# Ten of the MLP's half down projections as Strassen-like block products, and two weight sums made by adding loads

## The chip, the core and the metric

The kernel runs on one core of a Trainium2 chip. The metric is the device time of one execution in microseconds (us). The engines are TensorE (PE, with its weight loads as PEld), VectorE (DVE), ScalarE (ACT), GpSimd (POOL) and SyncE (SP), which starts most loads. All work from queues of their own and wait for each other through semaphores.

## What is computed

The reference is a decoder trunk of two layers on x of 512 positions by 1024 features, in float32:

```
for l in range(2):
    h = rms_norm(x, norm_mix_g[l])
    proj = h @ w_in[l]
    ... differential attention, short convolution, RWKV-7 ...
    x = x + mixed @ w_out[l]
    h = rms_norm(x, norm_mlp_g[l])
    x = x + square(relu(h @ w_mlp_up[l])) @ w_mlp_down[l]
return rms_norm(x, final_norm_g)
```

Only the MLP matters here: 1024 features up to 4096, squared ReLU, and down to 1024.

## The kernel before

Everything is kept transposed: a tile has 128 features on the partitions and the 512 positions along the free dimension. x is eight such tiles that stay in SBUF. To keep float32 precision each product is made of three matmuls: an operand is split into a high part (cast to fp32r) and a low part (the operand less the high part), and high times high, high times low and low times high are summed in PSUM. A weight chunk of 256 KB (four blocks of 128 by 128) is loaded by SP, its high part is cast by ScalarE (L346), its low part subtracted by VectorE (L347).

The MLP of a layer makes 32 "middle" tiles (up projection, ReLU, square) and sums them into x through 64 blocks of the down projection. Four middle tiles are made plainly (`up`), the other 28 in 14 pairs (`two`): a pair takes the tile pair, the two halves of the features and the two halves of the positions as a 2 by 2 block product and makes it from seven products instead of eight, each of 4 blocks by three matmuls of 256 columns, 84 matmuls in all. Products are summed in the PSUM tiles `pa`, `pb`, `pc`. The weight operands of the seven products are w11, w12, w22 and the sums s1 = w21 + w22, s2 = s1 - w11, s3 = w11 - w21, s4 = w12 - s2, made on VectorE (`sum_`, L1484 for the first pair and L1486). Each is split into `shi_p` (ScalarE, L1477) and `slo_p` (VectorE, L1478). The position operands are h's blocks and sums of them, made once a layer (`blocks`).

`square` turns a finished product c into a middle tile: VectorE takes ReLU and the scale of the norm into `r` (L1416), ScalarE squares it into `m` (L1418), ScalarE casts the high part `mh` (L1407), GpSimd subtracts the low part `ml` (L1408; VectorE for the first four).

`down(h, js)` takes the four middle tiles 4h to 4h+3 and four of the eight tiles of x (a half: js is 0 to 3 or 4 to 7): for each of them 4 blocks by three matmuls of 512 columns into a PSUM tile `dn` of two buffers (tag "mm"), and a VectorE add into x (L1554); 48 matmuls a half. After the pairs, one half follows each pair as soon as 4h+6 middle tiles stand, so the program alternates a pair and a half. That alternation is a period. PE's order is the program's; the order of the other engines' instructions is set by a scheduler from what they depend on and when they are due.

The kernel's weights for plain products go through a ring of three buffers (`weights`), and in the MLP every fourth chunk through a spare one.

The MLP starts behind the norm: GpSimd's `rrf` (L371) gives the norm's rates, which PE spreads over the partitions (`prbf`, L285).

Of the kernel before, what the change touches and what calls it, by code (L numbers as in the profile page):

```python
# [10 lines left out]
F32 = mybir.dt.float32  # L11
# [11 lines left out]
S = 512  # L23
P = 128
# [155 lines left out]
NG = NG_IN + NG_OUT + NG_UP + NG_DN  # L180

N_ONE = 4

WHOLE = 5
PT = 1
# [86 lines left out]
def tile_trunk(ctx: ExitStack, tc: tile.TileContext, xT, wts, prm_d, cst_d, lora_d, gup_d, lam_d, fin_d, hd_d, out):  # L272
# [29 lines left out]
    def psum(tag, bufs, name):  # L302
        return ps.tile([P, 512], F32, tag=tag, bufs=bufs, name=name)
# [167 lines left out]
    def last_group(fp, wbase, mids):  # L471
# [24 lines left out]
        def norm(half, sq):  # L496
# [23 lines left out]
            act.copy(rbs, rb[-1][:, :H])  # L520
            os_ = []
            for j in range(NK):
                o = fp.tile([P, H], F32, tag=("p1", "p5", "u2", "c1")[j // 2], bufs=2, name=f"o{half}_{j}")
# [42 lines left out]
    for l in range(L):  # L566
# [825 lines left out]
        acts = [inner[j] for j in range(NK)]  # L1392
        with ExitStack() as mx:
            fp = mx.enter_context(tc.tile_pool(name=f"fp{l}", bufs=1))
            spare[0] = fp
            RING = 10
            H = S // 2
            mids = []
# [3 lines left out]
            def kept(m):  # L1402

                i = len(mids)
                hi = fp.tile([P, S], F32R, tag="mh", bufs=RING, name=f"mh{l}_{i}")
                lo = fp.tile([P, S], F32R, tag="ml", bufs=RING, name=f"ml{l}_{i}")
                act.copy(hi, m)  # L1407
                (dve if i < 4 else pool).tensor_tensor(lo, m, hi.bitcast(F32), ALU.subtract)  # L1408
                mids.append((hi, lo))

            def square(cs, name):

                r = fp.tile([P, S], F32, tag="r", bufs=2, name=f"r{name}")
                for i, c in enumerate(cs):
                    q = slice(i * H, i * H + c.shape[1])
                    dve.scalar_tensor_tensor(r[:, q], c, 0.0, rs[:, q], ALU.max, ALU.mult)  # L1416
                m = fp.tile([P, S], F32, tag="m", bufs=3, name=f"m{name}")
                act.activation(m, r, AF.Square)  # L1418
                kept(m)

            def up(i):

# [23 lines left out]
            def blocks(q):  # L1446
                hi, lo = th[q] = [fp.tile([P, 4, H], F32R, tag=f"t{p}{q}", name=f"t{p}{l}_{q}") for p in ("hi", "lo")]
                for i in range(2):
                    u = slice(2 * i, 2 * i + 2)
                    t = fp.tile([P, 2, H], F32, tag="c0" if q == 1 else ("s3", "s4")[i], bufs=1 + (q == 1), name=f"t{l}_{q}_{i}")  # L1450
                    for k in (2 * i, 2 * i + 1):
                        b1, b2, o = bn[k], bn[k + 4], t[:, k % 2]
                        if q == 0:
                            dve.tensor_tensor(o, b1[:, 1], b1[:, 0], ALU.subtract)
                        elif q == 1:
                            dve.tensor_tensor(o, b2[:, 1], tb[0, i][:, k % 2], ALU.subtract)
                        elif q == 2:
                            dve.tensor_tensor(o, b2[:, 1], b1[:, 1], ALU.subtract)
                        else:
                            dve.tensor_tensor(o, b2[:, 0], tb[1, i][:, k % 2], ALU.subtract)  # L1460
                    tb[q, i] = t
                    act.copy(hi[:, u], t)
                    dve.tensor_tensor(lo[:, u], t, hi[:, u].bitcast(F32), ALU.subtract)

            def two(i0, i1):

# [1 line left out]
                wg = wbase + NG_IN + NG_OUT  # L1468

                def raw(i, a):  # L1470
                    t = fp.tile([P, 4, P], F32, tag="sraw", bufs=6, name=f"raw{n}_{i}_{a}")
# [8 lines left out]

                def sum_(name, a, b, op):
                    t = fp.tile([P, 4, P], F32, tag=name, name=f"{name}{n}")
                    if i0 == N_ONE and name in ("s1", "s3"):
                        dve.scalar_tensor_tensor(t, a, none, b, ALU.add, op)  # L1484
                    else:
                        dve.tensor_tensor(t, a, b, op)  # L1486
                    return t

                def small(name):
                    return fp.tile([P, H], F32, tag=name, bufs=2, name=f"{name}{n}")  # L1490
# [19 lines left out]
                w21 = raw(i1, 0)  # L1510
                w22 = raw(i1, 4)
# [4 lines left out]
                s2 = sum_("s2", s1, w11, ALU.subtract)  # L1516
# [3 lines left out]
                w12 = raw(i0, 4)  # L1520
                product(pc, both(w12, "p2"), blk(1, 0))
                dve.tensor_tensor(c0[:, :H], pc, p1, ALU.add)
                s3 = sum_("s3", w11, w21, ALU.subtract)
                product(pa, both(s3, "p7"), smm(2), False)
# [3 lines left out]
                s4 = sum_("s4", w12, s2, ALU.subtract)  # L1528
                product(pb, both(s4, "p3"), blk(1, 1), False)
                dve.tensor_tensor(c0[:, H:], pb, u2, ALU.add)  # L1530
                square([c0], f"{n}_0")
                product(pa, both(w22, "p4"), smm(3), False)
                square([pa, c1], f"{n}_1")
# [24 lines left out]

            for i in range(N_ONE):
                up(i)  # L1560
            for j in range(NK):
                by_gain(j)
            down(0, range(4))
# [82 lines left out]
```

## Time and profile before

| | |
|---|---|
| median of 3 runs | 1236.34 us (1236.31 to 1236.89) |
| the profiled execution's own time | 1238.42 us |
| its span | 1236.6 us |
| granted TensorE clock, mean | 0.998 |
| busy: PE, VectorE, ScalarE, GpSimd | 1226.2, 934.4, 693.0, 351.7 us |

The profile is one execution. A row of its timeline gives start and duration in us, the engine, the line, the operation, what is written and read by the program's names, the shape, and in brackets how long the engine had been idle and what ended that. The chain of waits follows back from the last instruction what released each step. A window gives the engines' busy time in a stretch. Line 285 is a helper through which all matmuls go, so PE's groups are told by tile.

### The profile page before, as it was taken

The page shows a single profiled execution, that of the slowest core. Times are in us where ns is not written, and L with a number is a line of the kernel's source. Part 1 is how long each engine was busy: PE and PEld are TensorE (multiplying, and loading weights), DVE is VectorE, ACT ScalarE, POOL GpSimd, SP SyncE. Part 2 cuts the span into 40 slices and gives each one's busy share as a digit, 9 for nine tenths or more (in the row PEclk, how much of TensorE's full clock was granted, in tenths as well). Part 3 has the DMA queues.
Part 4 walks back from the last instruction along what each step waited for, and adds up shares of the span by engine and source line. Part 5 has one row for each costly group of instructions (what it writes and reads, how often), then busy time and mean ns, then how long its engine had stood idle before and what let it go on. Part 6 is the DMA issues. An engine that isn't in the chain of part 4 may idle for free.

```text
span 1236.6 us, 25555 instructions
## 1 busy us (share of the span) xinstructions
PE 1226.2 (99%) x9730; PEld 1056.4 (85%) x9730; DVE 934.4 (76%) x1805; ACT 693.0 (56%) x1456; POOL 351.7 (28%) x450
## 2 busy tenths in 40 slices
PE   9999999999999999999999999999999999999997
PEld 7788788888999998989888888888889999998987
DVE  6787888879887676765666777887798867676753
ACT  6785655558455454544465657464775545454542
POOL 2263636341122111120035455464202211111111
PEclk9999999999999999999999999999999999999999
DMA  6523323124433323321235243232433333323121
GB/s 217 165 91 96 111 90 111 54 86 154 143 97 102 103 94 107 99 86 44 69 105 166 77 126 114 88 85 70 152 113 118 106 102 102 104 95 107 55 69 68
DMA packets 84266, 127.94 MB, mean 103 GB/s; under 512 B 21296, under 2 KB 25136, under 8 KB 84144
## 3 DMA queue, kind: packets, MB, share of 16 engines
q1 hardware_dynamic: 83424, 125.57, 32.5%
q8 instruction: 76, 1.25, 0.4%
q10 hardware_dynamic: 720, 0.75, 0.2%
q14 instruction: 46, 0.38, 0.1%
HBM read 117.11 MB, written 9.18 MB: 102 GB/s over the span
## 4 chain that ended last, share of the span: by engine, by line
PE 92%; DVE 2%; ACT 2%; DMA 1%; POOL 1%; issue 1%; SPq 0%; POOLq 0%; ACTq 0%; DVEq 0%
PE dn L285 25%; PE pj L285 21%; PE pa L285 13%; PE po L285 8%; PE pb L285 7%; PE dnF L285 4%; PE pc L285 3%; PE up L285 2%; PE sc L285 1%; PE ptt L290 1%; PE pg L285 1%; PE pyy L285 1%; PE pzw L285 1%; PE pst L285 1%; DMA raw<-wts 0%
## 5 line engine op out<-in xcount | busy, mean ns | idle before, releaser
L1408 POOL TENSOR_TENSOR ml<-m,mh 128x512 fp32r<-128x512 f32 x56 | 90.5, 1634 | 497.5 <-ACT mh L1407 356.5
L285 PE MATMUL dn<-mh,whi 128*128 128x512 f32 x448 | 175.5, 392 | 0.0
L285 PE MATMUL dn<-ml,whi 128*128 128x512 f32 x448 | 175.2, 391 | 0.1
L285 PE MATMUL dn<-mh,wlo 128*128 128x512 f32 x448 | 175.2, 391 | 0.0
L692 POOL TENSOR_TENSOR wlo<-raw,whi 128x512 fp32r<-128x512 f32 x84 | 111.5, 1328 | 210.4 <-ACT whi L680 167.2
L346 ACT CAST whi<-raw 128x512 fp32r<-128x512 f32 x126 | 77.9, 619 | 157.5 <-PE dn L285 147.8
L285 PE MATMUL pj<-ahim,whi 128*128 128x512 f32 x392 | 156.8, 400 | 0.0
L285 PE MATMUL pj<-ahim,wlo 128*128 128x512 f32 x392 | 156.4, 399 | 0.0
L285 PE MATMUL pj<-alom,whi 128*128 128x512 f32 x392 | 155.9, 398 | 0.0
L1554 DVE TENSOR_TENSOR x<-dn,x 128x512 f32<-128x512 f32 x108 | 74.5, 690 | 89.9 <-PE dn L285 89.8
L680 ACT CAST whi<-raw 128x512 fp32r<-128x512 f32 x142 | 87.7, 618 | 71.7 <-PE pj L285 27.5
L1477 ACT CAST shi_p<-s 128x512 fp32r<-128x512 f32 x112 | 69.4, 621 | 78.4 <-PE pa L285 61.9
L347 DVE TENSOR_TENSOR wlo<-raw,whi 128x512 fp32r<-128x512 f32 x126 | 97.3, 774 | 6.1 <-ACT whi L346 6.1
L285 PEld LDWEIGHTS dn<-mh,wlo 128*128 128x128 f32 x448 | 84.2, 188 | 18.5
L285 PEld LDWEIGHTS dn<-ml,whi 128*128 128x128 f32 x448 | 84.2, 188 | 17.7 <-DVE ml L1408 0.5
L285 PEld LDWEIGHTS dn<-mh,whi 128*128 128x128 f32 x448 | 84.1, 188 | 17.4
L285 PE MATMUL pa<-thi,shi_p 128*128 128x256 f32 x336 | 95.1, 283 | 0.0
L285 PE MATMUL pa<-tlo,shi_p 128*128 128x256 f32 x336 | 94.9, 282 | 0.0
L285 PE MATMUL pa<-thi,slo_p 128*128 128x256 f32 x336 | 94.1, 280 | 0.0
L1478 DVE TENSOR_TENSOR slo_p<-s,shi_p 128x512 fp32r<-128x512 f32 x112 | 77.6, 697 | 21.2 <-ACT shi_p L1477 18.4
L285 PEld LDWEIGHTS pj<-alom,whi 128*128 128x128 f32 x392 | 73.9, 188 | 14.0 <-issue 0.5
L285 PEld LDWEIGHTS pj<-ahim,wlo 128*128 128x128 f32 x392 | 73.8, 188 | 13.9 <-issue 0.2
(427 smaller groups left out, 3242.5 us busy)
## 6 DMA issues: line engine op xcount, KB each, us to landing
raw<-wts SPq DMA_DIRECT2D x389, 256.0 KB, 2.6
qs<-dqhi SPq DMA_DIRECT2D x24, 128.0 KB, 3.4
ks<-dkhi SPq DMA_DIRECT2D x24, 128.0 KB, 3.6
x<-xT SPq DMA_DIRECT2D x8, 256.0 KB, 5.0
dqhi<-qhi SPq DMA_DIRECT2D x6, 256.0 KB, 3.4
dqlo<-qlo SPq DMA_DIRECT2D x6, 256.0 KB, 3.4
dkhi<-khi SPq DMA_DIRECT2D x6, 256.0 KB, 3.1
dklo<-klo SPq DMA_DIRECT2D x6, 256.0 KB, 3.5
```

What stands on the lines that cost most here:

```text
L285: ins = nc.tensor.matmul(*a, **k)
L290: ins = nc.tensor.transpose(*a, **k)
L346: act.copy(hi[:, :n], raw[:, :n])
L347: (pool if a and lean[0] else dve).tensor_tensor(lo[:, :n], raw[:, :n], hi[:, :n].bitcast(F32), ALU.subtract)
L680: yield act.copy(hi[:, k0:k1], raw[:, k0:k1])
L692: yield eng.tensor_tensor(lo[:, k0:k1], raw[:, k0:k1], hi[:, k0:k1].bitcast(F32), ALU.subtract)
L1408: (dve if i < 4 else pool).tensor_tensor(lo, m, hi.bitcast(F32), ALU.subtract)
L1477: act.copy(hi, src)
L1478: dve.tensor_tensor(lo, src, hi.bitcast(F32), ALU.subtract)
L1554: dve.tensor_tensor(x[j], pt, x[j], ALU.add)
```

## The change

**The down halves.** In layer 0 the halves of h = 2, 4 and 6, and in layer 1 those of h = 2 and 4, become `quad`s, ten in all. A quad makes two pairs of x tiles; for a pair, the two x tiles, the two pairs of middle tiles (4h, 4h+2 and 4h+1, 4h+3) and the two halves of the positions are the 2 by 2 blocks, and seven products stand for eight, each of 2 blocks by three matmuls of 256 columns: 2 x 7 x 2 x 3 = 84 matmuls a quad. They run into PSUM tiles `qa`, `qb`, `qc`; after each product VectorE adds what stands in the tile into half of an x tile (L1587), and a later product goes on summing in `qa` or `qb`, so x is added to seven times a pair. The weight operands are w0 (a chunk of four blocks), two sums s12 and s34 built on VectorE from two chunks (four rows of 256 columns), and w22 (half a chunk), each split on ScalarE and VectorE (L1574).

**The middle tiles' blocks.** `turn_blocks` makes the sums of middle tiles that a quad needs, after the pair that makes them: four VectorE differences of 256 columns (L1554 to L1557: `ta`, `tb`), a low part of 512 (`dlo`, L1560) and two of 256 (`alof`, L1565), and the casts on ScalarE. It runs after six pairs in layer 0 and four in layer 1.

**The sums s1 and s3** of all 28 pairs are made by loads (`summed`): SP loads one chunk, and GpSimd issues a second load of another chunk into the same tile with an add. They are issued a pair ahead. A pair loads seven chunks then, before it was four. Signs are turned so that s2 and s4 are sums, and the second middle tile of a pair takes min for max.

**Buffers.** `square` writes `m` directly and squares in place, so `r` goes; `m` has four buffers; the spare weight buffers go; `sraw` has five buffers for six, `p5` one for two; the tile `o` of the norm before takes other places for j 2 and 3.

Three places where the order of instructions differs. The first is VectorE, layer 0, around the end of pair 10 and the first tile of the half h = 3. `r0_10` and `m0_10` are pair 10's middle tiles, `slo0_11` and `s30_12` belong to the next pairs, `wlo78_4` is a weight split. Before:

```order
L1416 SCALAR_TENSOR_TENSOR r0_10_0_5867<-c00_10_5743,rsf0_4121 128x512
L1416 SCALAR_TENSOR_TENSOR r0_10_1_5891<-pa0_10_5740,rsf0_4121 128x256
L1416 SCALAR_TENSOR_TENSOR r0_10_1_5891<-c10_10_5845,rsf0_4121 128x256
L1478 TENSOR_TENSOR slo0_11_p7_6070<-s30_11_6067,shi0_11_p7_6069 128x512
L1486 TENSOR_TENSOR s30_12_6307<-raw0_12_12_0_6224,raw0_12_26_0_6244 128x512
L1554 TENSOR_TENSOR x0_68<-dn0_3_0_5900,x0_68 128x512
L347 TENSOR_TENSOR wlo78_4_6144<-raw78_4_6141,whi78_4_6143 128x512
```

Now, with the blocks for h = 4:

```order
L1420 SCALAR_TENSOR_TENSOR m0_10_0_6037<-c00_10_5913,rsf0_4121 128x512
L1420 SCALAR_TENSOR_TENSOR m0_10_1_6060<-pa0_10_5910,rsf0_4121 128x256
L1420 SCALAR_TENSOR_TENSOR m0_10_1_6060<-c10_10_6015,rsf0_4121 128x256
L1494 TENSOR_TENSOR slo0_11_p2_6235<-raw0_11_11_4_6224,shi0_11_p2_6234 128x512
L1554 TENSOR_TENSOR ta0_4_0_6068<-m0_10_0_6037 128x256
L1494 TENSOR_TENSOR slo0_11_p7_6252<-s30_11_5979,shi0_11_p7_6251 128x512
L1555 TENSOR_TENSOR ta0_4_0_6068<-m0_10_1_6060,ta0_4_0_6068 128x256
L1556 TENSOR_TENSOR tb0_4_0_6069<-m0_10_1_6060,m0_10_0_6037 128x256
L1557 TENSOR_TENSOR tb0_4_0_6069<-m0_10_1_6060,ta0_4_0_6068 128x256
L1655 TENSOR_TENSOR x0_68<-dn0_3_0_6082,x0_68 128x512
```

Between the last middle row and the first add into x stand six rows now, two before; the split `p2`, ahead of the middle rows before, is one of them.

The second is VectorE in the first quad, h = 2, x tiles 0 to 3, layer 0, behind pair 8. `dn0_2` is the half's PSUM tile, `qa`, `qb` and `qc` the quad's. Before:

```order
L1416 SCALAR_TENSOR_TENSOR r0_8_1_5411<-c10_8_5365,rsf0_4121 128x256
L1478 TENSOR_TENSOR slo0_9_p7_5590<-s30_9_5587,shi0_9_p7_5589 128x512
L1486 TENSOR_TENSOR s30_10_5827<-raw0_10_10_0_5744,raw0_10_24_0_5764 128x512
L1554 TENSOR_TENSOR x0_68<-dn0_2_0_5420,x0_68 128x512
L347 TENSOR_TENSOR wlo78_0_5664<-raw78_0_5661,whi78_0_5663 128x512
L1554 TENSOR_TENSOR x1_69<-dn0_2_1_5440,x1_69 128x512
L347 TENSOR_TENSOR wlo79_0_5684<-raw79_0_5681,whi79_0_5683 128x512
L1554 TENSOR_TENSOR x2_70<-dn0_2_2_5460,x2_70 128x512
```

Now:

```order
L1420 SCALAR_TENSOR_TENSOR m0_8_1_5432<-c10_8_5387,rsf0_4121 128x256
L1587 TENSOR_TENSOR x0_68<-qa0_2_0_5466,x0_68 128x256
L1574 TENSOR_TENSOR wlo0_2_2d_5492<-rawq0_2_2_1_5470,whi0_2_2d_5491 128x256
L1587 TENSOR_TENSOR x0_68<-qc0_2_0_5468,x0_68 128x256
L1587 TENSOR_TENSOR x2_70<-qa0_2_2_5495,x2_70 128x256
L1494 TENSOR_TENSOR slo0_9_p1_5603<-raw0_9_9_0_5600,shi0_9_p1_5602 128x512
L1587 TENSOR_TENSOR x2_70<-qc0_2_2_5497,x2_70 128x256
L1587 TENSOR_TENSOR x1_69<-qb0_2_0_5467,x1_69 128x256
L1587 TENSOR_TENSOR x0_68<-qa0_2_0_5466,x0_68 128x256
L1499 TENSOR_TENSOR s20_9_5638<-s10_9_5348,raw0_9_9_0_5600 128x512
L1587 TENSOR_TENSOR x3_71<-qb0_2_2_5496,x3_71 128x256
L1494 TENSOR_TENSOR slo0_9_p5_5621<-s10_9_5348,shi0_9_p5_5620 128x512
```

Where adds into x and weight splits took turns, short adds from the quad's PSUM tiles now stand between the next pair's splits (`slo0_9`) and sums.

The third is GpSimd at the MLP's start in layer 0: the last sums of the norm (`accf`), `rrf`, a weight split and the first `ml`. Before:

```order
L763 TENSOR_TENSOR accf0_3865<-accf0_3865,sqf0_5_3994 128x512
L763 TENSOR_TENSOR accf0_3865<-accf0_3865,sqf0_6_4021 128x512
L371 TENSOR_TENSOR rrf0_4086<-rsx_4087,ones1_80 128x4
L692 TENSOR_TENSOR wlo36_4_4118<-raw36_4_4073,whi36_4_4116 128x512
L1408 TENSOR_TENSOR ml0_4_4512<-m0_4_0_4509,mh0_4_4511 128x512
```

Now:

```order
L768 TENSOR_TENSOR accf0_3865<-accf0_3865,sqf0_6_4021 128x512
L1479 DMA s10_4_4230<-wts 128x512
L1479 DMA s30_4_4233<-wts 128x512
L373 TENSOR_TENSOR rrf0_4086<-rsx_4087,ones1_80 128x4
L1479 DMA s10_5_4448<-wts 128x512
L697 TENSOR_TENSOR wlo36_4_4118<-raw36_4_4073,whi36_4_4116 128x512
L1479 DMA s30_5_4451<-wts 128x512
L1479 DMA s10_6_4686<-wts 128x512
L1479 DMA s30_6_4689<-wts 128x512
L1479 DMA s10_7_4844<-wts 128x512
L1412 TENSOR_TENSOR ml0_4_4513<-m0_4_0_4509,mh0_4_4512 128x512
```

The adding loads of pairs 4 to 7 stand ahead of the first `ml`, two of them ahead of `rrf`. Each waits for the plain load into its tile.

The diff's core:

```diff
+DN_QUADS = (((2, 0), (2, 1), (4, 0), (4, 1), (6, 0), (6, 1)), ((2, 0), (2, 1), (4, 0), (4, 1)))
...
+            def summed(p, name):
+                if p < N_TWO:
+                    i0, i1 = N_ONE + p, N_ONE + N_TWO + p
+                    t = sums[p, name] = fp.tile([P, 4, P], F32, tag=name, bufs=2, name=f"{name}{l}_{i0}")
+                    of = [wts[wbase + NG_IN + NG_OUT + i, :, a * P:(a + 4) * P] for i, a in ((i1, 0), (i1, 4) if name == "s1" else (i0, 0))]
+                    nc.sync.dma_start(t.rearrange("p k c -> p (k c)"), of[0])
+                    pool.dma_start(t.rearrange("p k c -> p (k c)"), of[1], accum_op=ALU.add)
...
-                s1 = sum_("s1", w21, w22, ALU.add)
+                s1 = sums[i0 - N_ONE, "s1"]
...
+            def turn_blocks(h, k, b1, b2):
...
+                dve.tensor_tensor(a[:, 0], b1[:, H:], b1[:, :H], ALU.subtract)
+                dve.tensor_tensor(a[:, 1], b2[:, H:], a[:, 0], ALU.subtract)
+                dve.tensor_tensor(b[:, 0], b2[:, H:], b1[:, H:], ALU.subtract)
+                dve.tensor_tensor(b[:, 1], b2[:, :H], a[:, 1], ALU.subtract)
...
+                for step in ((0, 1), (2, 3), (4, 5), (6,)):
+                    for j, w0, s12, s34, w22, (pa, pb, pc) in ab:
+                        for c in step:
+                            if c == 0:
+                                product(pa, w0, (0, 2), blk(0, 0), True, False)
+                                add(j, 0, pa)
...
+                            elif c == 3:
+                                product(pa, s12, (2, 3), trn(1), False, False)
+                                add(j, 1, pa)
...
             def down(h, js):
+                if (h, js[0] // 4) in DN_QUADS[l]:
+                    quad(h, js[0] // 4)
+                    return
...
-                two(N_ONE + p, N_ONE + N_TWO + p)
+                ms = two(N_ONE + p, N_ONE + N_TWO + p)
+                hk = divmod(N_ONE // 2 + p, 2)
+                if any(q[0] == hk[0] for q in DN_QUADS[l]):
+                    turn_blocks(*hk, *ms)
```

More of the change, by code (lines that the diff above doesn't have):

```diff
@@ L522, in norm @@
             for j in range(NK):
-                o = fp.tile([P, H], F32, tag=("p1", "p5", "u2", "c1")[j // 2], bufs=2, name=f"o{half}_{j}")
+                if j // 2 == 1:
+                    o = fp.tile([P, H], F32, tag=("dhi", "dlo")[half] + str(j % 2), name=f"o{half}_{j}")
+                else:
+                    o = fp.tile([P, H], F32, tag=("p1", "", "u2", "c1")[j // 2], bufs=2, name=f"o{half}_{j}")
                 if j in ((2, 5) if half else (2, 5, 6, 7)):
@@ L1449, in blocks @@
                     u = slice(2 * i, 2 * i + 2)
-                    t = fp.tile([P, 2, H], F32, tag="c0" if q == 1 else ("s3", "s4")[i], bufs=1 + (q == 1), name=f"t{l}_{q}_{i}")
+                    tag, bufs = ("c0", 2) if q == 1 else (("s3", 2), ("s4", 1))[i]
+                    t = fp.tile([P, 2, H], F32, tag=tag, bufs=bufs, name=f"t{l}_{q}_{i}")
                     for k in (2 * i, 2 * i + 1):
@@ L1470, in raw @@
                 def raw(i, a):
-                    t = fp.tile([P, 4, P], F32, tag="sraw", bufs=6, name=f"raw{n}_{i}_{a}")
+                    t = fp.tile([P, 4, P], F32, tag="sraw", bufs=5, name=f"raw{n}_{i}_{a}")
                     nc.sync.dma_start(t.rearrange("p k c -> p (k c)"), wts[wg + i, :, a * P:(a + 4) * P])
@@ L1482, in sum_ @@
                     t = fp.tile([P, 4, P], F32, tag=name, name=f"{name}{n}")
[L1483 to L1486, printed above, removed]
+                    dve.tensor_tensor(t, a, b, op)
                     return t
                 def small(name):
-                    return fp.tile([P, H], F32, tag=name, bufs=2, name=f"{name}{n}")
+                    return fp.tile([P, H], F32, tag=name, bufs=2 - (name == "p5"), name=f"{name}{n}")
                 def product(pt, w, moving, first=True):
@@ L1520, in two @@
                 w12 = raw(i0, 4)
+                w22 = raw(i1, 4)
+                for s in ("s1", "s3"):
+                    summed(i0 - N_ONE + 1, s)
                 product(pc, both(w12, "p2"), blk(1, 0))
                 dve.tensor_tensor(c0[:, :H], pc, p1, ALU.add)
-                s3 = sum_("s3", w11, w21, ALU.subtract)
-                product(pa, both(s3, "p7"), smm(2), False)
+                product(pa, both(sums[i0 - N_ONE, "s3"], "p7"), smm(2), False)
                 c1 = small("c1")
@@ L1560, in tile_trunk @@
                 up(i)
+            for s in ("s1", "s3"):
+                summed(0, s)
             for j in range(NK):
```

91 lines of the change are left out of this document (76 added, 15 removed).

## The prediction

> **What bounds the kernel now.** I read the page's busy times and its chain of waits first, then the chain itself through one period of the MLP in either layer, then that period engine by engine. The engines (name, busy us, share), the chain's share by engine, and the kernel's loads (count, size, median us to landing):
>
> ```profile
> PE 1226.2 (99%) x9730; PEld 1056.4 (85%) x9730; DVE 934.4 (76%) x1805; ACT 693.0 (56%) x1456; POOL 351.7 (28%) x450
> PE 92%; DVE 2%; ACT 2%; DMA 1%; POOL 1%; issue 1%; SPq 0%; POOLq 0%; ACTq 0%; DVEq 0%
> raw<-wts SPq DMA_DIRECT2D x389, 256.0 KB, 2.6
> ```
>
> TensorE is the bound: every matmul removed shortens the end, as long as no other engine makes it wait. The chain (start, us, engine, tile) in a period of layer 0 and one of layer 1:
>
> ```profile
> 396.69 11.04 PE dn L285 x48
> 407.73 1.42 PE pa L285 x12
> ...
> 416.30 1.43 PE pa L285 x12
> 417.73 11.04 PE dn L285 x48
> ```
> ```profile
> 1004.42 10.93 PE dn L285 x48
> 1015.34 1.42 PE pa L285 x12
> ...
> 1025.34 10.93 PE dn L285 x48
> ```
>
> A half `down` is 48 matmuls and 11.04 us (10.93 in layer 1). A pair of up tiles is 84 matmuls and 417.73 − 407.73 = 10.00 us. Nothing else stands in the chain: PE never waits here. The same period by engine (stretch, busy us and instructions of PE, PEld, DVE, ACT, POOL, then clock, DMA share, GB/s), and who waits for whom (us, times, longest):
>
> ```profile
> 386.69:407.73 21.04, 21.04 (x135) 19.02 (x134) 15.28 (x25) 10.12 (x20) 3.40 (x2) 1.00 0.32 102
> ```
> ```profile
> DVE x L1554 <- PE dn L285: 89.8, 70, 2.3
> ```
>
> VectorE is busy 15.28 of 21.04 us and waits for PE in its `x` adds. It is second in line, and the change gives it more to do.
>
> **What the change removes.** Ten halves of 48 matmuls of 512 columns become ten of 84 matmuls of 256 columns, three to a k, the same shape as a pair of up tiles. So a quad costs 10.00 us: 1.04 less than a half in layer 0, six times, and 0.93 less in layer 1, four times. 6 × 1.04 + 4 × 0.93 = 9.96 us off PE. That term is nearly certain; what follows is what the other engines give back.
>
> **VectorE's ledger.** Its rows around the seam of a pair and the half after it (start, duration, operation, and in brackets idle time before it):
>
> ```profile
> 396.29 0.68 DVE L1478 TENSOR_TENSOR slo_p<-raw,shi_p 128x512 fp32r<-128x512 f32 x1
> 396.89 0.69 DVE L1416 SCALAR_TENSOR_TENSOR r<-c,rsf 128x512 f32<-128x512 f32 x1
> 397.50 0.42 DVE L1416 SCALAR_TENSOR_TENSOR r<-pa,rsf 128x256 f32<-128x256 f32 x1
> 397.83 0.42 DVE L1416 SCALAR_TENSOR_TENSOR r<-c,rsf 128x256 f32<-128x256 f32 x1
> 398.16 0.69 DVE L1478 TENSOR_TENSOR slo_p<-s,shi_p 128x512 fp32r<-128x512 f32 x1
> 398.88 0.69 DVE L1486 TENSOR_TENSOR s<-raw,raw 128x512 f32<-128x512 f32 x1
> 399.49 0.69 DVE L1554 TENSOR_TENSOR x<-dn,x 128x512 f32<-128x512 f32 x1
> 400.10 1.18 DVE L347 TENSOR_TENSOR wlo<-raw,whi 128x512 fp32r<-128x512 f32 x1
> 402.29 0.69 DVE L1554 TENSOR_TENSOR x<-dn,x 128x512 f32<-128x512 f32 x1 [1.01 <-PE dn L285]
> ```
>
> Rows that wait for nothing start 0.605 us apart at 512 columns (396.29, 396.89, 397.50) and 0.335 at 256. A period had 20 rows of 512 and 5 of 256, 13.8 us. Without the sums s1 and s3 it has 12.6. A period that turns blocks gets six rows of 256 and one of 512 more, 2.6: 15.2 of 21.04. A period with a quad loses four `x` adds and four weight splits (8 × 0.605) and gets, for two block pairs, 6 rows of 512 and 24 of 256: 12.6 − 4.84 + 11.67 = 19.4 of 20.0 us. VectorE has time in the one and almost none in the other, so order decides.
>
> **The ten turns.** `dn` has two PSUM buffers, so the first `x` add must end before the third tile starts, two tiles after the half began: 2 × 11.04 / 4 = 5.52 us. The last middle row's slot ended at 398.16, 1.47 us after the half's start; one split of 0.60 that stood ahead of those rows now follows them, so 0.87 to 1.47. From there the order has two splits and four block rows, 2 × 0.605 + 4 × 0.335 = 2.55, then the add, 0.69: done at 4.11 to 4.71, a slack of 0.81 to 1.41; I take 1.11. Into this stretch fall GpSimd's two `ml`, here beside the same instructions elsewhere (GpSimd's rows, then VectorE's at the second place):
>
> ```profile
> 399.04 3.40 POOL L1408 TENSOR_TENSOR ml<-m,mh 128x512 fp32r<-128x512 f32 x2 [17.63 <-PE dn L285]
> 566.71 2.55 POOL L1408 TENSOR_TENSOR ml<-m,mh 128x512 fp32r<-128x512 f32 x2 [16.98 <-ACT mh L1407]
> ```
> ```profile
> 954.85 1.79 DVE L1486 TENSOR_TENSOR s<-raw,raw 128x512 f32<-128x512 f32 x1
> 956.56 1.78 DVE L1486 TENSOR_TENSOR s<-raw,s 128x512 f32<-128x512 f32 x1
> ```
>
> They start at 399.04, 2.35 into the half, and take 2.55 when nothing disturbs them. At 399.04 they took 3.40, and the split under them 1.18 in place of 0.69; the `x` add at 399.49, with one operand in PSUM, kept its 0.69. Where VectorE had only rows with both inputs in SBUF, two rows took 1.79 and 1.78: 2.2 lost. Before, one such row met them; in a turn all six rows around them are of that kind. The bounds for a turn are thus 0.49, less than the slack, and 2.2; I take 1.9, near the second, because its rows are the like ones, a little less because the first block row can miss them. 1.9 − 1.11 = 0.8 us of PE per turn, 8 us for ten. The ends are 0 and 2.2 − 0.81 = 1.4 each, 14 in all.
>
> The Trainium skill, page "SBUF — State Buffer", section "Who interferes with whom", says that VectorE with two SBUF inputs contends with a GpSimd instruction that reads SBUF, that the loser blocks for a whole instruction, and that one SBUF input does not contend. The rows agree on who meets whom: 1.79 for two SBUF inputs, 0.69 for the add. By a full block of both `ml` (2.55) a turn would cost 1.4 and the ten 14 us, the upper end above; the measured rows decide, so the sum keeps 8.
>
> **The ten quads.** PE reuses a bank of `qa` or `qb` only after VectorE has added it to `x`; those adds are queued behind splits and sums of the next pair. 19.4 plus the one meeting of 0.49 is 19.9 of 20.0: no stall; 19.4 plus 2.2 is 21.6: 1.6 a quad, 16 in all. Fourteen of the rows are adds from PSUM, like the one that kept 0.69, so I take 0.15 a quad, 1.5.
>
> **The two starts.** The first pair's sums s1 and s3 are no longer made on VectorE, but are a load and a second load that GpSimd starts when the first has landed. GpSimd's `rrf`, which feeds PE, now stands behind two of these. Rows of the start (layer 0 twice, then layer 1):
>
> ```profile
> 282.90 1.46 POOL L371 TENSOR_TENSOR rrf<-rsx,ones 128x4 f32<-128x4 f32 x1 [3.85 <-DVE none L1434]
> ```
> ```profile
> 287.20 0.49 PE L285 MATMUL prbf<-cst,rrf 128*128 128x128 f32 x3
> ```
> ```profile
> 887.83 5.84 DMA raw<-wts
> ```
> ```profile
> 893.79 1.33 DVE L1484 SCALAR_TENSOR_TENSOR s<-raw,none,raw 128x512 f32<-128x512 f32 x1 [2.46 <-DMA raw<-wts]
> ```
> ```profile
> 913.68 0.62 DVE ml L1408
> 914.29 0.04 issue
> 914.34 6.88 PE dn L285 x29
> ```
>
> `rrf` ended at 284.36 and was needed at 287.20, 2.8 later; it was released 3.85 idle us after its predecessor, long enough for a landing of 2.6. In layer 1 a load took 5.84, VectorE waited 2.46 for it, and the last `ml` released PE at 914.29 with nothing to spare. A second load adds 2.6 to 5.84 behind the first, but the splits of the plain weights can run meanwhile, and the two sums are gone (two rows of 1.33 or less). I take 0.5 a layer, 1 us; the ends are 0 and 5.84 − 1.33 = 4.5 in layer 1 alone. The Trainium skill, page "DMA: Bandwidth & Descriptors", section "Anatomy of one DMA — SWDGE (gpsimd) path", gives 2.0 us and bytes over 436 GB/s, about 2.6 us by estimate; no run here shows a load from GpSimd's queue.
>
> **At nothing.** Issue on GpSimd: 17.63 us idle ahead of `ml` cover it. Three more chunks a pair: DMA share 0.32, by 7 chunks in place of 4 beside the half's 4, about 0.44. Three weight buffers for four: two tiles of 5.5 us cover a split of 0.60 and a cast. ScalarE: 10.12 of 21.04, some casts more.
>
> **The sum.** −9.96 + 8 + 1.5 + 1 = +0.5 us. The profiled execution took 1238.42 us for its span of 1236.6; the median is 1236.34, so a difference is carried over to the median: 1236.9. A difference under about 0.2%, 2.5 us, can't be told from none.
>
> **Rivals.** A, the forecast: 0.42. Its own range has turns at 0.5 to 1.1 and the small terms at 0 to 3 each, 1231 to 1243: faster 0.08, same 0.24, slower 0.10.
> B, the meetings don't reach PE: faster. If `ml` starts later than the block rows (GpSimd's order has it behind adding loads now) or earlier, or loses to VectorE instead of holding it (it did lose 0.85 of 3.40 at 399.04), the turns cost nothing: −9.96 to −9, 1226.4 to 1227.4. For it: only 0.8 us too much per turn. Against it: `ml` is released by the squares that release the block rows. 0.35.
> C, VectorE becomes the bound in the quads: slower. Its place is the run of `x` adds and splits. If rows wait for what they need and so cost their full 0.69 and 0.42, 16 rows of 512 and 29 of 256 take 23.2 us against 20.0: 3.2 × 10 − 10 = +22, 1258. It decides where over two fifths of the rows do so (1.6 of 3.8 us is a quad's gain and its room). Against it: the rows above follow at 0.605. 0.11.
> D, adding loads come late: slower. A sum is loaded a pair ahead, 21 us, and two landings take 5.2 to 11.7; if GpSimd issued them 0.8 us too late in each of 28 pairs, +22 − 10, 1248. 0.08.
> That the change doesn't do what it says is excluded by PE's order: 84 matmuls of 256 columns stand for 48 of 512. The rest, 0.04, is slower.
> Faster is 0.35 + 0.08 = 0.43, same 0.24, slower 0.10 + 0.11 + 0.08 + 0.04 = 0.33. The range, 1226.4 to 1248, takes in A's unknown costs at their ends (−9.96 + 14 + 3 + 4.5 = +11.5) and B, and leaves out C, the rest and half of D.
>
> **What would show it.** Right: a quad of 10.0 us in the chain; in the ten turns a VectorE row of over 1.1 us beside `ml` and a gap of PE before `dn`'s third tile, ended by an `x` add; no gap elsewhere over 0.3. B: no such gaps. C: waits of PE for `x` adds inside quads, VectorE without idle time there. D: shi or s2 waiting for a DMA. It is wrong if a quad takes over 10.3, or if PE waits in other periods.

## The result, and the profile after

The changed kernel takes 1258.56 us (median of 4 runs, 1256.52 to 1260.38) against 1236.32 before: ratio 1.0179, 95% interval 1.0161 to 1.0198. It is 1.8% slower; the forecast was no difference, and the time lies beyond the range. The profiled execution took 1257.57 us with a span of 1255.6, so it shows 19.0 of the 22.2 us.

The page after: busy times, the chain by engine, and the loads into the sums and into a quad's chunks (queue, count, size, median us to landing):

```profile
PE 1223.7 (97%) x10090; PEld 1066.1 (85%) x10090; DVE 1004.1 (80%) x2039; ACT 721.7 (57%) x1526; POOL 390.4 (31%) x506
PE 74%; DVE 12%; DMA 5%; issue 5%; ACT 3%; POOL 1%; POOLq 0%; ACTq 0%; DVEq 0%
s<-wts SPq DMA_DIRECT2D x56, 256.0 KB, 3.2
s<-wts POOLq DMA_DIRECT2D x56, 256.0 KB, 5.2
rawq<-wts SPq DMA_DIRECT2D x40, 256.0 KB, 3.0
```

PE fell from 92% of the chain to 74%: in its place stand VectorE, loads and their issue. The busy times hardly tell this; VectorE has 80%.

To see where, I took for each pair, half and quad the time from its first matmul to the first of the next stage. Undisturbed, a pair takes 10.00 us and a half 10.93 in either layer; for a quad I set 10.00. The third pair of each layer takes 10.42 in every kernel, before included, and is set at that. The table has the sums over what is longer than that, and for the two starts of the MLP the shift of the first pair against before (for layer 1 counted from the end of layer 0's MLP), in us, good to about 0.1:

| kernel | start 0 | start 1 | quads | halves | pairs |
|---|---|---|---|---|---|
| before | 0 | 0 | - | 1.5 | 0.0 |
| after | 0.7 | 4.2 | 12.8 | 11.9 | 0.0 |

The rows add up: 0.7 + 4.2 + 12.8 + (11.9 - 1.5) less the ten quads' 10 x 0.93 is 18.8 us, and the last group of the down projection starts at 1200.50 where it started at 1181.67. So the gain came, and three places gave back more than it. Of the 11.9 in the halves, 11.3 stand behind the ten turns; 0.6 is the half behind layer 1's first pair, which follows no turn.

**The start of layer 1.** The chain after, and VectorE's rows:

```profile
893.96 3.66 DMA s<-wts
897.66 0.61 issue
898.28 7.51 DMA s<-wts
905.81 0.04 DVE s L1499
```
```profile
899.06 0.43 DVE L1459 TENSOR_TENSOR t<-bn 128x256 f32<-128x256 f32 x1 [0.88 <-ACT bn L1447]
905.81 0.75 DVE L1499 TENSOR_TENSOR s<-s,raw 128x512 f32<-128x512 f32 x1 [6.32 <-DMA s<-wts]
```

The sum s2 needs s1. s1 now comes of two loads one behind the other, and the second took 7.51 us. VectorE's queue has s2 early, so VectorE stands 6.32 us with the rows for the position blocks and the middle tiles behind it. Before, its wait there was 2.46.

**The turns.** VectorE, GpSimd and PE around the half after one of them (pair 11, layer 0):

```profile
464.36 0.42 DVE L1554 TENSOR_TENSOR ta<-m 128x256 f32<-128x256 f32 x1
464.69 0.42 DVE L1599 TENSOR_TENSOR s2q<-s2q,rawq 128x256 f32<-128x256 f32 x1
465.06 1.49 DVE L1555 TENSOR_TENSOR ta<-m,ta 128x256 f32<-128x256 f32 x1
466.47 1.51 DVE L1556 TENSOR_TENSOR tb<-m,m 128x256 f32<-128x256 f32 x1
467.90 0.41 DVE L1557 TENSOR_TENSOR tb<-m,ta 128x256 f32<-128x256 f32 x1
468.24 0.68 DVE L1655 TENSOR_TENSOR x<-dn,x 128x512 f32<-128x512 f32 x1
```
```profile
464.62 3.07 POOL L1412 TENSOR_TENSOR ml<-m,mh 128x512 fp32r<-128x512 f32 x2 [0.84 <-issue]
```
```profile
468.97 0.50 PE L287 MATMUL dn<-mh,whi 128*128 128x512 f32 x1 [0.95 <-DVE x L1655]
```

The two block rows beside `ml` take 1.49 and 1.51 instead of 0.42, the first add comes behind them, and PE starts the third tile late. That half took 12.19 us, 1.26 too many. Of the ten halves behind turns nine are longer like this; the one behind pair 10 in layer 0 kept its 10.93.

**The second quads.** VectorE in front of the second quad of h = 2, and SyncE's issue of the chunk it waits for:

```profile
414.25 0.42 DVE L1602 TENSOR_TENSOR s4q<-rawq,s2q 128x256 f32<-128x256 f32 x1
...
419.13 0.42 DVE L1598 TENSOR_TENSOR s2q<-rawq 128x256 f32<-128x256 f32 x1 [1.28 <-DMA rawq<-wts]
```
```profile
414.69 0.33 SPq L1594 DMA_DIRECT2D rawq<-wts  x1
```

PE inside that quad:

```profile
423.75 0.38 PE L287 MATMUL qa<-dhi,shi_4b 128*128 128x256 f32 x1 [0.36 <-DVE x L1587]
```

A quad takes four weight chunks, the ring has three buffers, and `s4q` is the last reader of the first two. The fourth load is issued right behind it and lands 4 us later; then the sums, casts and splits of the quad's second pair of tiles come in one bunch with the middle tiles' rows, and the adds into x that PE waits for stand behind them. In layer 0 the quads behind pairs 8 and 9 took 10.54 and 11.79 us, those behind pairs 12 and 13 10.79 and 11.60, and the last two, behind pairs 16 and 17, 10.52 and 10.04. The last one has no pair behind it.

### The profile page after: what moved, and what is told of

Same layout as the page of the kernel before. It is cut to its first block, busy times and chain, and to the rows that moved or that the text cites. A ratio compares the mean times of both kernels' runs of the same rounds, so it can differ in the third digit from the quotient of the medians.

```text
span 1255.6 us, 26902 instructions
## 1 busy us (share of the span) xinstructions
PE 1223.7 (97%) x10090; PEld 1066.1 (85%) x10090; DVE 1004.1 (80%) x2039; ACT 721.7 (57%) x1526; POOL 390.4 (31%) x506
## 4 chain that ended last, share of the span: by engine, by line
PE 74%; DVE 12%; DMA 5%; issue 5%; ACT 3%; POOL 1%; POOLq 0%; ACTq 0%; DVEq 0%
PE pj L287 21%; PE pa L287 10%; PE dn L287 10%; PE po L287 8%; PE pb L287 5%; PE dnF L287 3%; PE pc L287 3%; PE qa L287 2%; DMA s<-wts 2%; DVE x L1587 2%; DVE slo_p L1494 2%; DMA rawq<-wts 2%; PE sc L287 1%; PE ptt L292 1%; DVE m L1420 1%
## 5 line engine op out<-in xcount | busy, mean ns | idle before, releaser
L1412 POOL TENSOR_TENSOR ml<-m,mh 128x512 fp32r<-128x512 f32 x56 | 82.4, 1516 | 204.6 <-ACT mh L1411 118.1
L1479 POOL DMA_DIRECT2D s<-wts x56 | 51.1, 923 | 291.4 <-DVE slo_p L1494 83.6
L685 ACT CAST whi<-raw 128x512 fp32r<-128x512 f32 x142 | 87.6, 618 | 72.6 <-PE pj L287 27.0
L287 PE MATMUL dn<-mh,whi 128*128 128x512 f32 x288 | 113.7, 395 | 10.5 <-DVE x L1655 9.1
L287 PE MATMUL dn<-ml,whi 128*128 128x512 f32 x288 | 112.6, 391 | 0.7 <-DVE ml L1412 0.7
L287 PE MATMUL dn<-mh,wlo 128*128 128x512 f32 x288 | 112.2, 390 | 0.0
L348 ACT CAST whi<-raw 128x512 fp32r<-128x512 f32 x86 | 53.2, 619 | 80.2 <-PE dn L287 53.4
L287 PEld LDWEIGHTS pj<-ahim,whi 128*128 128x128 f32 x392 | 74.0, 189 | 13.6 <-issue 0.3
L287 PEld LDWEIGHTS dn<-mh,whi 128*128 128x128 f32 x288 | 54.0, 188 | 26.1 <-DVE x L1655 6.9
L349 DVE TENSOR_TENSOR wlo<-raw,whi 128x512 fp32r<-128x512 f32 x86 | 68.3, 801 | 9.7 <-ACT whi L348 9.5
L1493 ACT CAST shi_p<-raw 128x512 fp32r<-128x512 f32 x84 | 52.1, 620 | 33.5 <-PE pb L287 17.6
```

The lines of the kernel that those rows point to most:

```text
L287: ins = nc.tensor.matmul(*a, **k)
L348: act.copy(hi[:, :n], raw[:, :n])
L349: (pool if a and lean[0] else dve).tensor_tensor(lo[:, :n], raw[:, :n], hi[:, :n].bitcast(F32), ALU.subtract)
L685: yield act.copy(hi[:, k0:k1], raw[:, k0:k1])
L1479: pool.dma_start(t.rearrange("p k c -> p (k c)"), of[1], accum_op=ALU.add)
L1493: act.copy(hi, src)
```

## The experiments

Theory P: three places with three causes, the start, the turns and the quads' chunks. Rival V: VectorE has too many rows in the quad periods, rival C of the prediction, which gave 1258 and so fits the time. Rival S: the adding loads cost in every pair.

The same table for the experiments, with the median and its ratio to before:

| kernel | start 0 | start 1 | quads | halves | pairs | us | ratio (95%) |
|---|---|---|---|---|---|---|---|
| e1 adding loads only | 1.8 | 5.6 | - | 0.0 | 0.2 | 1244.56 | 1.0063 (1.0048 to 1.0078) |
| e2 with turns, no quads | 2.5 | 6.0 | - | 11.7 | 1.0 | 1257.50 | 1.0164 (1.0147 to 1.0181) |
| e3 quads, no turns | 0.2 | 4.0 | 14.9 | 0.6 | 0.0 | 1248.09 | 1.0089 (1.0061 to 1.0117) |
| e4 four banks | 1.5 | 4.2 | 12.4 | 1.7 | 3.1 | 1250.64 | 1.0112 (1.0097 to 1.0127) |
| e5 fourth chunk | 1.3 | 3.6 | 2.4 | 19.6 | 0.0 | 1252.56 | 1.0127 (1.0103 to 1.0150) |
| e6 first sums | -2.0 | -0.1 | 12.0 | 11.9 | 0.7 | 1251.31 | 1.0120 (1.0105 to 1.0135) |
| e7 turn after | 0.5 | 3.6 | 11.6 | 7.8 | -0.1 | 1254.82 | 1.0149 (1.0132 to 1.0166) |
| e8 e5, e6 and e7 | -2.0 | 0.4 | 2.4 | 6.6 | 0.6 | 1236.76 | 1.0003 (0.9993 to 1.0012) |
| e9 e8 and e4 | -1.8 | 2.3 | 2.4 | 0.0 | 1.4 | 1231.92 | 0.9957 (0.9941 to 0.9973) |
| e10 e8, ml on VectorE | -2.4 | 0.3 | 2.4 | 0.0 | 0.4 | 1230.07 | 0.9944 (0.9931 to 0.9957) |
| e11 e1 and e6 | -1.0 | 1.0 | - | -0.2 | 1.7 | 1238.56 | 1.0012 (1.0003 to 1.0021) |
| e12 e10, no adding loads | -2.8 | 0.0 | 2.4 | 0.5 | 0.0 | 1228.34 | 0.9929 (0.9915 to 0.9942) |

The columns are each from one profiled execution, the medians from 4 to 11 runs. An execution can lie off its median: e5's took 1254.67 us, e7's 1251.30. In five of them the records show stretches of 3.4 us at a granted clock of 0.50 inside the MLP: one in start 1 of e1, e2 and e4 each, worth up to 1.7 us there; one in a quad of e3 that took 14.16 us, worth 1.5; and two in halves of e5, worth 1.6 each. Before and after have none there.

### e1: the adding loads alone

```diff
-DN_QUADS = (((2, 0), (2, 1), (4, 0), (4, 1), (6, 0), (6, 1)), ((2, 0), (2, 1), (4, 0), (4, 1)))
+DN_QUADS = ((), ())
```

Expected: 

> The set of quads is empty in both layers, so no quad is made and no blocks are turned; the adding loads and the changes to buffers stay. Theory P (three separate places: the start of the MLP, the turns, the quads' loads): only the starts remain, 0.7 us in layer 0 and 4.8 in layer 1, less about 0.1 us for each plain half of layer 0 that takes 10.93 instead of 11.04: 1236.3 + 5.5 - 1.6, about 1240. Rival V (VectorE has too many rows in the quads, and nothing else matters): no difference, 1236. Rival S (adding loads slow every pair): over 1245.

Measured 1244.56, 7.8 over before, more than the 4 expected. In the profile all of it is in the starts, 1.8 and 5.6, up to 1.7 of the second at the lower clock; the other pairs and halves run undisturbed, and layer 0's halves take 10.93. The chain at the start of layer 1:

```profile
892.87 7.17 DMA s<-wts
```

So the adding loads cost nothing that shows in the 26 later pairs, and the first ones alone make the kernel slower by a third of the whole loss.

### e2: turns without quads

```diff
-                if (h, js[0] // 4) in DN_QUADS[l]:
+                if False:
```

Expected: 

> As the change, but the ten halves are made plainly, 48 matmuls of 512 columns; the blocks are turned all the same and nobody reads them. Theory P: the kernel with the adding loads alone plus ten stalls of about 1.1 us at the third tile of the half after a turn, 11 us: about 1251. Rival V: within 2 us of the kernel with the adding loads alone.

Measured 1257.50, 12.9 over e1. The halves lose 11.7 us with no quad in the kernel, all but about 0.5 of it behind the ten turns. The block rows (ten of each; shortest, median, longest in ns):

```profile
L1555 DVE TENSOR_TENSOR ta<-m,ta x10: 420/1151/1154, 359.6 to 1088.5; 128x256 f32<-128x256 f32 x10
```
```profile
L1557 DVE TENSOR_TENSOR tb<-m,ta x10: 421/1518/1521, 360.3 to 1089.9; 128x256 f32<-128x256 f32 x10
```

Which of the block rows is held differs from the change, that two are held doesn't: 1151 - 420 and 1518 - 420 ns is 1.8 us.

### e3: quads without turns

```diff
-                    turn_blocks(*hk, *ms)
+                    turned.update({(i, k): (th[i][0][:, k], th[i][1][:, k]) for i in range(4) for k in range(2)})
```

Expected: 

> As the change, but no blocks are turned: the quads read slices of the up projection's position blocks instead, so that their sums leave out the middle tiles' differences. Theory P: the adding loads alone, less 10.0 for the quads' matmuls, plus the stalls seen in the quads, 12.8: about 1243, the halves after the former turns at 10.93. Rival V: VectorE is relieved only outside the quads, so the quads still stall and the time stays near 1256.

Measured 1248.09, 3.5 over e1: in the profile the quads' matmuls save 9.3, their stalls cost 14.9 (1.5 of it at the lower clock), and the starts come 3.2 earlier than in e1. The halves behind the former turns take 10.93; the 0.6 is again the half behind layer 1's first pair. Turns and quads are two causes, since each stays when the other goes.

### e4: four PSUM buffers for a half

```diff
-                    pt = psum("mm", 2, f"dn{l}_{h}_{j}")
+                    pt = psum("mm" if j % 4 < 2 else "at", 2, f"dn{l}_{h}_{j}")
```

Expected: 

> As the change, but the third and fourth tile of a plain half are summed in the two PSUM buffers of the tag at, so the third tile doesn't wait for the first add into x. Theory P: VectorE's rows beside ml keep their 1.5 us, but PE doesn't wait for them: 11 us less than the change, about 1247, the halves after turns at about 11.0. Rival V: VectorE's lateness is only handed on to the next pair, where the splits come late: less than 4 us gained.

Measured 1250.64, 7.9 less than the change. The halves' 11.9 went to 1.7, but 3.1 came up in the pairs, 1.09 in each of two of them. ScalarE in front of the first of these:

```profile
390.45 0.62 ACT L1573 CAST whi_2a<-rawq 128x512 fp32r<-128x512 f32 x1 [4.79 <-DMA rawq<-wts]
```

The load of that chunk had waited 6.0 us for a split of VectorE's to free its buffer, and the pair's own cast and copy, for which PE waits, stand behind this cast. So VectorE's lateness is in part handed on, through a load and ScalarE's queue. The stall at the third tile was what the turns cost; most of the lateness behind it is caught up.

### e5: a buffer for the fourth chunk

```diff
-                    r0, r1 = [wp.tile([P, 4, P], F32, tag="raw", bufs=WB, name=f"rawq{n}_{c}") for c in range(2)]
+                    r0, r1 = [(fp.tile([P, 4, P], F32, tag="sraw", bufs=5, name=f"rawq{n}_{c}") if i and c else
+                               wp.tile([P, 4, P], F32, tag="raw", bufs=WB, name=f"rawq{n}_{c}")) for c in range(2)]
```

Expected: 

> As the change, but the last of a quad's four weight chunks goes into the up pairs' chunk ring (sraw) instead of being the fourth in a ring of three, so its load doesn't wait until the quad's first pair of tiles has used the first two chunks. Theory P: the second quads of h = 2 and 4, 11.8, 11.6, 13.2 and 12.3 us long, come down to the 10.5 of the first ones, 6 to 7 us in all: about 1252. Rival V (VectorE has too many rows there, whatever the loads do): the second quads stay over 11.5, 1257 or more.

Measured 1252.56, as theory P had it, but not by its sum. All ten quads came to 10.2 to 10.3, first ones too: 12.8 to 2.4. The halves took 7.7 of it back: two halves after a turn took 14.84 and 15.04. The chain in the first of these:

```profile
443.53 0.42 DVE ta L1555
443.95 0.34 DVE tb L1556
444.29 3.25 DVE tb L1557
447.54 0.61 DVE x L1656
448.15 0.04 issue
```

A single row of 256 columns took 3.25 us; it was held through both `ml`. PE waited 2.0 us for the add behind it, and then its clock fell (stretch, busy us of PE, PEld, DVE, ACT, POOL, then granted clock, DMA share, GB/s):

```profile
449.50:452.90 3.40, 3.40 (x10) 2.66 (x9) 1.90 (x4) 0.61 (x1) 0.00 (x0) 0.51 0.67 158
```

A matmul of 512 columns followed the last after 0.43 us there, and after 0.23 around it, which is 1.6 us of this half. The half of 15.04 shows the same, 0.50 behind a wait of 2.2 us. So 3.2 of the 7.7 is the lower clock, not VectorE. Why these rows were held longer here than in the change was not tried.

### e6: the first pair's sums on VectorE

```diff
+                if i0 == N_ONE:
+                    w21, w22 = raw(i1, 0), raw(i1, 4)
+                    for name, b in (("s1", w22), ("s3", w11)):
+                        t = sums[0, name] = fp.tile([P, 4, P], F32, tag=name, bufs=2, name=f"{name}{n}")
+                        dve.scalar_tensor_tensor(t, w21, none, b, ALU.add, ALU.add)
```

Expected: 

> As the change, but the first pair's s1 and s3 in each layer are summed on VectorE from plainly loaded chunks, as before the change; the other 26 pairs keep their adding loads. Theory P: VectorE no longer stands 6.3 us at the head of its queue for the adding load at the start of layer 1's MLP, and the up stage and first half there come back to before: 5 to 7 us less than the change, about 1252. Rival S (GpSimd's load issues delay rrf and the adding loads of later pairs cost as well): less than 2 us.

Measured 1251.31, 7.3 less than the change. Start 1 is back at before; start 0 is 2.0 earlier than before, for a reason that was not tried. The quads and halves keep 12.0 and 11.9.

### e7: turning after the half

```diff
-                if any(q[0] == hk[0] for q in DN_QUADS[l]):
-                    turn_blocks(*hk, *ms)
                 if len(mids) >= 4 * h + 6 and h < 2 * N_KG - 2 * (l == L - 1):
                     down(h, range(4 * half, 4 * half + 4))
                     h, half = h + half, 1 - half
+                if any(q[0] == hk[0] for q in DN_QUADS[l]):
+                    turn_blocks(*hk, *ms)
```

Expected: 

> As the change, with the blocks turned after the half in the program instead of ahead of it. VectorE's rows are the same in number; only the first add into x now stands ahead of the last two block differences and the low parts. Theory P: the stall of 1.2 us at the third tile after each turn goes, since 1.44 and 0.34 us of rows move behind the add: 9 to 11 us less, about 1249. Rival V: VectorE is as late as before and hands it on to the next pair: less than 4 us gained.

Measured 1254.82, only 3.7 less. The halves after the second turn of an h came to 11.06 to 11.09, those after the first still took 11.5 to 12.7. e8, with the same order, shows why (VectorE, then GpSimd):

```profile
522.32 0.42 DVE L1559 TENSOR_TENSOR ta<-m 128x256 f32<-128x256 f32 x1
523.02 3.09 DVE L1560 TENSOR_TENSOR ta<-m,ta 128x256 f32<-128x256 f32 x1 [0.28 <-ACT m L1421]
526.04 0.68 DVE L1661 TENSOR_TENSOR x<-dn,x 128x512 f32<-128x512 f32 x1
```
```profile
522.97 2.85 POOL L1412 TENSOR_TENSOR ml<-m,mh 128x512 fp32r<-128x512 f32 x2
```

I had counted one `ml` to a row. This row began at 523.02, just after the first `ml` had begun, and came free only behind the second: it lost 2.7 us, and the add behind it as much. My expectation fell on that; the place was right.

The turn of pair 11 above went otherwise, and the two `ml` taken singly show a difference (first that turn, then e8):

```profile
464.62 1.64 POOL L1412 TENSOR_TENSOR ml<-m,mh 128x512 fp32r<-128x512 f32 x1 [0.84 <-issue]
466.23 1.47 POOL L1412 TENSOR_TENSOR ml<-m,mh 128x512 fp32r<-128x512 f32 x1
```
```profile
522.97 1.62 POOL L1412 TENSOR_TENSOR ml<-m,mh 128x512 fp32r<-128x512 f32 x1
524.22 1.60 POOL L1412 TENSOR_TENSOR ml<-m,mh 128x512 fp32r<-128x512 f32 x1
```

Where the second begins as the first ends (466.23 against 466.26), a row gets in between them. Where it begins earlier (524.22 against 524.59), the row is held through both.

### e8: the three mends together

Expected: 

> The three mends together: the fourth chunk in the pairs' ring, the first pair's sums on VectorE, blocks turned after the half. Theory P: 1258.6 - 6.5 - 6 - 10 = 1236, level with the kernel before, since first quads still lose 0.5 us each. If the three places were one and the same shortage of VectorE, the gains would overlap: 1245 or more.

Measured 1236.76, level with before. The three alone gave 6.0 + 7.3 + 3.7 = 17.0 and together 21.8, so their gains don't overlap, as those of one shortage would; the halves' 19.6 in e5 are 6.6 here.

### e9 and e10: the held row made harmless, and made impossible

e9 is e8 with e4's edit. e10 is e8 with the turned tiles' `ml` on VectorE:

```diff
-                (dve if i < 4 else pool).tensor_tensor(lo, m, hi.bitcast(F32), ALU.subtract)
+                (dve if i < 4 or any(q[0] == i // 4 for q in DN_QUADS[l]) else pool).tensor_tensor(lo, m, hi.bitcast(F32), ALU.subtract)
```

Expected of e9: 

> The three mends and, besides, the third and fourth tile of a plain half in the PSUM buffers of the tag at. In the kernel with the three mends, five halves after a turn still take 11.7 to 12.4 us, each behind one row of VectorE that is blocked. Theory P: PE no longer waits for that row's successor, the first add; 6.6 us of the halves' excess go, 1 or 2 are handed on to the next pair: 1231 to 1232. Rival V (VectorE has no time to make up for it): 1235 or more.

Expected of e10: 

> The three mends, and the low parts ml of the middle tiles that are turned are made on VectorE instead of GpSimd: VectorE gets two more rows of 512 columns, 1.2 us, in each turn period, and no GpSimd instruction reads beside it there. Theory P (VectorE is blocked by ml, it isn't short of time): no row of VectorE over 0.8 us in the turns, the halves after turns near 10.95, 6.6 us less than with the three mends: about 1230. Rival V (VectorE has too many rows): the halves after turns get longer, 1240 or more.

Measured 1231.92 and 1230.07. In both no half loses anything. In e10 VectorE does more, and its rows are short again:

```profile
L1560 DVE TENSOR_TENSOR ta<-m,ta x10: 417/421/425, 355.1 to 1063.1; 128x256 f32<-128x256 f32 x10
```

And through the first two quads and the pair between them (stretch, busy us of PE, PEld, DVE, ACT, POOL):

```profile
394.21:424.69 30.48, 30.48 (x254) 30.11 (x253) 30.48 (x69) 19.00 (x35) 7.25 (x6) 1.00 0.44 124
```

VectorE is busy for all of the 30.48 us, and rival V falls, since no half got longer. PE's busy time shows no wait, but its weight loads do. VectorE, the weight load of the fifth product of the first quad, and all such waits of the kernel (us, times, longest):

```profile
398.57 1.11 DVE L1499 TENSOR_TENSOR s<-s,raw 128x512 f32<-128x512 f32 x1
399.60 0.41 DVE L1592 TENSOR_TENSOR x<-qa,x 128x256 f32<-128x256 f32 x1
```
```profile
400.07 0.19 PEld L287 LDWEIGHTS qa<-ahif,shi_0c 128*128 128x128 f32 x1 [0.17 <-DVE x L1592]
```
```profile
PEld qa L287 <- DVE x L1592: 1.9, 10, 0.2
```

A split or sum took 1.11 us instead of 0.69 beside an `ml` that e10 leaves on GpSimd, and the add that PE needs stands behind it. This comes once in each of the ten quads, in e5 and e12 too, and is the 0.24 that a quad takes over 10.00.

### e11: adding loads without the start, and without quads

e1's and e6's edits.

Expected: 

> No quads and no turns, the adding loads for all pairs but the first of each layer, whose sums are made on VectorE; the buffers as in the change. Theory P: the start costs nothing, VectorE has two rows fewer a pair, and the plain halves of layer 0 take 10.93 instead of 11.04: 1234 to 1235. Rival S (adding loads cost in every pair): over 1238.

Measured 1238.56, 4 us over the expectation and 0.1% over before. To the last group the profile is level with before (1181.64 against 1181.67): 1.7 gained in halves, the starts level, 1.7 lost in pairs, 1.3 of them in the first pair of layer 1. There ScalarE stood 4.69 us at a cast that waited for its load, with the pair's copy behind it, and PE waited 1.0 for that copy. The end behind the last group is 0.9 longer. What delays that load and the end wasn't tried. The time itself lies in rival S's range, over 1238; against S speak the other 27 pairs, of which one alone is longer, by 0.5. Two VectorE rows less in each pair bring nothing where PE waits for none of them.

### e12: no adding loads

e6's edit for all pairs, on top of e10.

Expected: 

> The three mends and ml on VectorE in the turns, and in all pairs s1 and s3 summed on VectorE from plainly loaded chunks: no adding loads at all. VectorE gets two rows of 512 columns more a pair. Theory P: where rows follow at 0.605 us, a period with a quad then has 19.4 + 1.2 = 20.6 us of VectorE work for 20.2 us of PE, so quads with a pair behind them come to 10.5 to 11.5 us from 10.25, and other periods don't change: 2 to 8 us more than with the adding loads, 1232 to 1238. Rival: if the adding loads only cost, with GpSimd's issues and a share of the transfers, the time is at or under 1230.

Measured 1228.34, where I expected 2 to 8 more than e10; that is the rival's time, at or under 1230. It is 1.7 less than e10, but the two intervals overlap: neither a cost nor a gain of the adding loads is shown, and a gain of 2 us is excluded. GpSimd's `ml` keep their median of 1.38 us, the quads 10.24, and VectorE in a stretch of quads and in layer 0's MLP:

```profile
395.00:425.00 30.00, 30.00 (x250) 29.63 (x249) 29.92 (x67) 17.46 (x34) 5.48 (x4) 1.00 0.28 89
300.00:620.00 320.00, 320.00 (x2217) 297.57 (x2216) 292.88 (x573) 176.99 (x336) 30.38 (x25) 1.00 0.31 100
```

With the sums back on VectorE it has 292.88 of 320.00 us, and PE waits for it as in e10, 0.24 a quad. My ledger by period was too strict; I take it that a period over its time borrows from the next, which no run shows by itself. This version beats both kernels, by 0.7% against before.

## Why the prediction was wrong, point by point

In its own terms the sum came out as -10.0 (the gain) + 11.3 (the turns) + 12.8 (the quads) + 4.9 (the starts) - 0.9 (plain halves) + 0.7 (the half behind layer 1's first pair and the last two of layer 0) = 18.8 us.

**The gain** was right. A quad is 10.00 us of matmuls, as put, against 11.04 and 10.93. Not foreseen: plain halves of layer 0 take 10.93 too after the change, 0.9 us in all; e1 shows it without a quad, and which of the buffer changes does it was not tried.

**The turns**: the mechanism and the place were right, the term mis-sized. Put at 0.8 each, 8 in all, with ends 0 and 14; the ten halves behind them lost 11.3 (e2: 11.1). I let two meetings cost 1.9, a little less than in the rows of layer 1's start, and a slack of 1.11. The blocked row loses up to both `ml`, 2.7 us, in e8's row. The Trainium skill, page "SBUF — State Buffer", section "Who interferes with whom", calls the ports that VectorE and GpSimd share an exclusive lock, and says of VectorE's two-port modes that whoever comes second is blocked for the whole instruction. Read for these rows too, that gave 14, nearer to 11.3 than my 8. The trace goes further: 3.09 us for a row of 0.42, held through two `ml`.

**The quads** are the step that failed. I put 0.15 each, 1.5 in all, from the meetings and VectorE's adds; they cost 12.8. The meetings come to nearly that, 0.24 each or 2.4 in all in e5 and e10, as e10's rows show. The other 10.4 stood under "At nothing", with the weight buffers: "Three weight buffers for four: two tiles of 5.5 us cover a split of 0.60 and a cast." That holds for a half, whose tiles take one chunk after the other. A quad holds two chunks until two sums of four are made, takes four, and there are three buffers: the fourth load waited for VectorE, and VectorE then for the load. e5 took just that away, and the quads came from 12.8 to 2.4.

**The starts**: mechanism right, size wrong. Put at 1 for both, ends 0 and 4.5 in layer 1; the profile has 0.7 and 4.2, and e6 gets 7.3 us back by median. I let the splits run meanwhile; but s2 stands at the head of VectorE's queue, and behind it nothing runs for 6.32 us. The adding load took 7.51 there and 5.2 in the median. The estimate of 2.6 us from the Trainium skill's page "DMA: Bandwidth & Descriptors", section "Anatomy of one DMA — SWDGE (gpsimd) path", doesn't hold for an adding load; no run here shows a plain one from GpSimd's queue.

**The rivals.** C gave 1258, which is the time, and is not the cause. One of its signs showed, waits of PE for `x` adds inside quads. The other did not: VectorE stood idle for the load in front of the second quad, and its rows inside mostly followed each other at 0.60 and 0.33 us. e5 takes no row off VectorE and ends all but 0.24 of a quad's waits, and e10 and e12 keep that though VectorE is full in their quads. D, adding loads too late, is half right: at the two starts, where there is no pair of lead, and in no other place that e1 shows. B's time, 1226 to 1227, is nearly what e12 shows, by other means: the meetings do reach PE, unless GpSimd doesn't read there.

## What to carry to other kernels

Where an engine is the bound at 99% and work is taken off it, go through each tile's buffers for the new step: how many it holds at once, who frees them, and which queue stands behind that. A time that fits a rival does not prove the rival; the table of stages told three causes apart that the sum had hidden, and each could be mended for itself. An engine that is busy all the time is not yet the bound: what counts is which of its rows PE waits for, and what stands ahead of that row. PE's busy time can hide such a wait; the waits of its weight loads show it.

## What the runs showed of the hardware

- A VectorE row with both inputs in SBUF, started behind the first of two GpSimd `ml` in a row, was held through one (1.49 us for 0.42 in the change) or through both (3.09 in e8, 3.25 in e5). In the traces of all 14 kernels 134 rows of over 0.9 us were held through one: there the second `ml` began at most 0.08 us before the first ended, or after it. 66 were held through both: there it began 0.14 to 0.40 us before. What makes the second begin early was not tried.
- An adding load of 256 KB issued by GpSimd took 5.2 us in the median to land, 7.51 at the longest wait shown, against 3.2 for the plain load into the same tile; its 56 issues kept GpSimd for 51.1 us, 0.92 each.
- In e5 the granted clock fell to 0.51 for 3.4 us, 1.2 us after a PE wait of 2.0 us had ended, and to 0.50 behind one of 2.2, as in e3 behind one of 2.4; matmuls of 512 columns took 0.63 us there for 0.39. Behind a wait of 1.8 us in e5 it did not fall.
